# Retention stage of a decoder trunk: order and queues of its loads, and the place of the first output tile of its projection

## The chip, the core and the metric

The kernel runs on one core of one Trainium2 chip. The metric is the device time of one execution in microseconds (us), lower is better; a median of several executions is compared with that of the kernel before.

## The reference

One inference step of two layers, a retention layer and a sliding-window attention layer, for a new prompt of 1024 tokens (model width 1024) and eight decode tokens with stored states. The change lies in the retention layer: 4 heads, query and key width 256, value width 512, cut into 8 chunks of 128 tokens. Everything is float32.

```python
def retention_scan(q, k, v, S0):
    ...
    dmask = jnp.where(dist[None] >= 0, jnp.exp(log_g[:, None, None] * jnp.maximum(dist, 0.0)[None]), 0.0)
    cross_decay = jnp.exp(log_g[None, :] * (idx[:, None] + 1.0))
    k_decay = jnp.exp(log_g[None, :] * (C - 1.0 - idx[:, None]))
    chunk_decay = jnp.exp(log_g * C)
    ...
    def step(S, inp):
        qc, kc, vc = inp
        inner = jnp.einsum('bthd,bshd->bhts', qc, kc) * dmask[None]
        o = jnp.einsum('bhts,bshe->bthe', inner, vc) \
            + jnp.einsum('bthd,bhde->bthe', qc, S) * cross_decay[None, :, :, None]
        S_new = S * chunk_decay[None, :, None, None] \
            + jnp.einsum('bshd,bshe->bhde', kc * k_decay[None, :, :, None], vc)
        return S_new, o
    ...

def retention_layer(x, S0, g_norm, w_in, g_out, w_out):
    ...
    proj = h @ w_in
    q, k, v, gate = jnp.split(proj, [RET_QK, 2 * RET_QK, 2 * RET_QK + RET_V], axis=-1)
    ...
    o, S = retention_scan(q, k, v, S0)
    o = rmsnorm(o, g_out.reshape(RET_HEADS, RET_DV)).reshape(B, L, RET_V)
    o = o * jax.nn.silu(gate)
    return x + o @ w_out, S.astype(S0.dtype)
```

The attention layer that follows, and the decode tokens (one token each, with their own state), are left out here; neither is computed in another way after the change.

## The kernel before, in words

Float32 products run on TensorE as three matmuls each: every operand is split into a high part (a copy rounded to the matrix format, by ScalarE or VectorE) and a low part (the rest, by VectorE or GpSimd), and hi x hi, hi x lo and lo x hi are summed in PSUM. So each loaded tile has a conversion in front of its matmuls.

**Stage A** computes the input projection of the retention layer, set by set (queries, keys, values, gate, per head), and writes the results to three DRAM scratch tensors: `qks` (queries and keys, transposed), `vsc` (values) and `gsc` (gate). The output tiles pass through a small ring of SBUF buffers, `ring(key)`, with the keys `p`, `x`, `c`, `w` (the names `evp`, `evx`, `evc`, `evw` in the profile); `out_of` (line 346) takes one. The last set is a gate set; its spills are the last writes to `gsc`. The decode tokens' state work runs alongside. The order of ACT, DVE, POOL and SP is written by hand: work is entered with a time or a slot number and sorted, and `later(n, fn)` puts `fn` at slot `n` of the list. `b_first` (line 750) is entered five slots before the end and issues the first loads of stage B.

**Stage B** is the chunkwise retention. Its 32 steps are 4 heads x 8 chunks, two heads side by side: `steps` runs over the pair (0, 1), chunk by chunk, head by head, then over the pair (2, 3). So step 14 and 15 are the last chunk of heads 0 and 1, and steps 16 and 17 the first of heads 2 and 3; this is called the change of heads. A step `i` is spread over several iterations of the loop at line 1010:

- loads, all on SP (the SyncE queue): `b_q` (queries and keys, into ring `p`), `b_v` (values, ring `x`), `b_g` (gate, rings `c` and `w` by turns), 256 KB each; for step i+2 in iteration i, `b_q` ahead of the other work, `b_v` and `b_g` behind it
- `b_qk` (PE): scores and the transposed keys into the PSUM tile `tr`; in iteration i-1
- `others`: ScalarE's `kh`, `sTh`, `vh` (high parts of keys, scores, values), VectorE's `kl`, `sT`, `qh`, GpSimd's `vl`, `sTl`, `ql` for step i+1; the state's parts `Sh` (ACT, line 933) and `Sl` (DVE) from PSUM for step i-1; the norm of the output of step i-1 (ACT square, DVE and POOL for the root, DVE `on`); the gated output of step i-2 (`og`, then its high part into `A_hi` or `B_hi` and its low part)
- `b_mm` (PE, line 905): the matmuls of step i: the state (`S`, two PSUM tiles per head, lines from 913) and the output (`po`, up to line 926)
- `b_tr` (PE): four transposes of the normalised output `on` of step i-1 (printed as L100, the line of the helper)

At the last chunk of a head `b_Sh` writes the scaled state into an SBUF tile `sf` and stores it to the output on SP (line 938). The output norm's gain row of a head, `gbh`, is loaded by `gbl` (line 989) on SP into one of two buffers: heads 0 and 1 ahead of the loop together with the masks `M23`, heads 2 and 3 in iterations 14 and 15. In iteration 4 four VectorE operations (lines 1025 to 1028) multiply the decode tokens' output by their gate and split it.

**The output projection** (`ro_part`, `ro_finish`, from line 1114) follows. Output tile `ft` is 128 of the 1024 output columns for 512 tokens (`gi` 0) or 256 and 264 tokens (`gi` 1 and 2); it sums over 16 blocks of 128 rows of `w_out_ret`, in two halves `kh`, with 3 matmuls per block. The weights come in slots of 1024 x 256, so one slot serves one half of two neighbouring output tiles: `wslot` (line 1057) loads it on SP in two loads of 512 KB into `wr`, DVE makes `wh` (line 1071), POOL `wl` (line 1072); there are three slots' buffers and `ro_ahead` says how far ahead they are made. `ro_finish` loads the residual rows `xr` on SP, adds them on PE by four transposes into the same PSUM tile, and ACT copies the sum out and squares it for the next norm. The PSUM and SBUF pools of stage B are closed before the projection begins, so its buffers lie in the same memory, and a first write into such a buffer waits for the last reader of what lay there.

## Time and profile before

| what | value |
|---|---|
| median of 3 runs | 1365.36 us (1364.91 to 1365.54) |
| profiled execution, its own time | 1366.37 us |
| its span in the profile | 1364.6 us |
| mean granted TensorE clock | 0.99 |
| PE busy | 1313.3 us (96%) |
| DVE, ACT, POOL busy | 699.7, 629.5, 708.1 us |
| DMA | 186.63 MB, 137 GB/s over the span |

Durations in the text are of the profiled execution and count from the span's start. The engines are PE (TensorE matmul), PEld (its weight loads, beside PE), DVE (VectorE), ACT (ScalarE), POOL (GpSimd) and SP (SyncE, which only issues DMAs here; SPq and ACTq are the queues' issue instructions). In a row of the timeline stand the start, the duration, the engine, the line, the operation, the output and the inputs, and, in brackets, how long the engine had been idle before and what ended that. In a row of the windows stand the stretch and its length, then the busy time of PE (with the number of matmuls that began), PEld, DVE, ACT and POOL, the granted clock as a share of full speed, the DMA engines' share, and GB/s. A row of the groups ends in the busy time, the mean duration in ns and the idle time ahead.

### The profile page before, as it was taken

Reading aid. Unit: us, or ns where it says so; the run is one execution under the profiler, and the core shown is the slowest. Engines: PE = TensorE matmul, PEld = TensorE weight load, DVE = VectorE, ACT = ScalarE, POOL = GpSimd, SP = SyncE. Lnnn points to the kernel's source line nnn. Section 1 sums busy time; section 2 is a strip of 40 time slices with the busy share of each in tenths; the row PEclk is TensorE's granted clock in tenths of the full one; section 3 lists DMA queues with packets and bytes.
Section 4 is the critical chain, followed back from the end, with each engine's and each line's share of the span. In section 5 each row is a group of like instructions: output and inputs, shape, how many; then the busy total and the mean of one; then the engine's idle time right before and its main releaser. Section 6 shows DMA issues by size and latency. Waiting matters only on the chain.

```text
span 1364.6 us, 25935 instructions
## 1 busy us (share of the span) xinstructions
PE 1313.3 (96%) x9661; PEld 1225.7 (90%) x9661; DVE 699.7 (51%) x1361; ACT 629.5 (46%) x1561; POOL 708.1 (52%) x825
## 2 busy tenths in 40 slices
PE   6999999999999999897979999998999999999998
PEld 6999999999999999686868889997898999998998
DVE  6943655556556653675751112335555555669321
ACT  5532544545456543575740112244466666656311
POOL 6653525435445443697986553544476666545000
PEclk9999999999999999899989999999999999999999
DMA  6314677577667743565545354442112111103523
GB/s 219 102 55 144 209 234 220 173 225 232 197 213 219 219 147 98 182 174 197 169 148 170 113 158 129 127 129 79 47 47 63 48 43 34 48 30 100 166 81 82
DMA packets 192659, 186.63 MB, mean 137 GB/s; under 512 B 12581, under 2 KB 172381, under 8 KB 192517
## 3 DMA queue, kind: packets, MB, share of 16 engines
q1 hardware_dynamic: 155840, 148.87, 35.9%
q10 hardware_dynamic: 36692, 36.11, 8.5%
q8 instruction: 76, 1.25, 0.4%
q14 instruction: 51, 0.41, 0.1%
HBM read 128.56 MB, written 57.41 MB: 136 GB/s over the span
## 4 chain that ended last, share of the span: by engine, by line
PE 85%; DVE 5%; DMA 3%; POOL 3%; issue 2%; ACT 1%; SPq 0%; ACTq 0%; POOLq 0%; DVEq 0%
PE b L330 7%; PE b L332 7%; PE b L331 7%; PE pj L1082 6%; PE pj L1084 6%; PE pj L1083 6%; PE pj L1133 5%; PE pj L1131 4%; PE pj L1132 4%; PE b L323 4%; PE b L324 4%; PE b L325 4%; PE tr L100 4%; PE o L1546 2%; PE sc L1508 1%
## 5 line engine op out<-in xcount | busy, mean ns | idle before, releaser
L330 PE MATMUL b<-xh,woh 128*128 128x258 f32 x784 | 223.3, 285 | 0.0
L332 PE MATMUL b<-xh,wol 128*128 128x258 f32 x784 | 221.6, 283 | 0.0
L331 PE MATMUL b<-xl,woh 128*128 128x258 f32 x784 | 221.2, 282 | 0.0
L1082 PE MATMUL pj<-A_hi,wh 128*128 128x384 f32 (+1 forms) x512 | 178.1, 348 | 0.0
L1084 PE MATMUL pj<-A_hi,wl 128*128 128x384 f32 (+1 forms) x512 | 164.7, 322 | 0.0
L1083 PE MATMUL pj<-A_lo,wh 128*128 128x384 f32 (+1 forms) x512 | 164.6, 321 | 0.0
L330 PEld LDWEIGHTS b<-xh,woh 128*128 128x128 f32 x784 | 148.0, 189 | 4.1 <-issue 2.5
L331 PEld LDWEIGHTS b<-xl,woh 128*128 128x128 f32 x784 | 148.8, 190 | 0.0
L332 PEld LDWEIGHTS b<-xh,wol 128*128 128x128 f32 x784 | 148.1, 189 | 0.0
L221 POOL TENSOR_TENSOR wol<-raw,woh 128x512 fp32r<-128x512 f32 x52 | 68.5, 1325 | 139.1 <-ACT woh L216 138.3
L1072 POOL TENSOR_TENSOR wl<-wr,wh 128x1024 fp32r<-128x1024 f32 (+1 forms) x60 | 115.2, 1932 | 44.0 <-DVE wh L1071 21.7
L324 PE MATMUL b<-wol,xh 128*128 128x256 f32 x448 | 126.1, 281 | 0.4 <-DVE wol L221 0.4
L323 PE MATMUL b<-woh,xh 128*128 128x256 f32 x448 | 126.3, 282 | 0.0
L325 PE MATMUL b<-woh,xl 128*128 128x256 f32 x448 | 125.7, 281 | 0.0
L1082 PEld LDWEIGHTS pj<-A_hi,wh 128*128 128x128 f32 x512 | 97.0, 189 | 10.1 <-issue 9.4
L1083 PEld LDWEIGHTS pj<-A_lo,wh 128*128 128x128 f32 x512 | 97.2, 190 | 0.0
L1084 PEld LDWEIGHTS pj<-A_hi,wl 128*128 128x128 f32 x512 | 96.6, 189 | 0.0
L1523 POOL TENSOR_TENSOR s<-s,sm 128x512 f32<-128x512 f32 x64 | 68.9, 1077 | 48.4 <-DVE sm L1522 46.5
L323 PEld LDWEIGHTS b<-woh,xh 128*128 128x128 f32 x448 | 84.3, 188 | 2.5 <-issue 1.2
L324 PEld LDWEIGHTS b<-wol,xh 128*128 128x128 f32 x448 | 84.3, 188 | 0.8 <-DVE wol L221 0.8
L325 PEld LDWEIGHTS b<-woh,xl 128*128 128x128 f32 x448 | 84.3, 188 | 0.0
L1515 ACT ACTIVATE s<-s,mx 128x257 f32<-128x257 f32 x128 | 64.0, 502 | 31.6 <-DVE mx L1513 27.9
(357 smaller groups left out, 3569.6 us busy)
## 6 DMA issues: line engine op xcount, KB each, us to landing
raw<-in_w_in_ret_dram ACTq DMA_DIRECT2D x44, 512.0 KB
st<-in_state_ret_dram SPq DMA_DIRECT2D x64, 256.0 KB
out_dram<-st SPq DMA_DIRECT2D x64, 256.0 KB
wr<-in_w_out_ret_dram SPq DMA_DIRECT2D x32, 512.0 KB
wr<-in_w_in_swa_dram SPq DMA_DIRECT2D x18, 512.0 KB
vb<-vscr SPq DMA_DIRECT2D x64, 128.0 KB
evp<-qks SPq DMA_DIRECT2D x32, 256.0 KB
evx<-vsc SPq DMA_DIRECT2D x32, 256.0 KB
```

The lines of the kernel that those rows point to most:

```text
L221: eng.tensor_tensor(lo, src_of(s, name, sub), hi.bitcast(F32), SUB)
L323: mm(dst, xh, wh, start=a and i == 0, stop=False, skip_group_check=True)
L324: mm(dst, xh, wl, start=False, stop=False, skip_group_check=True)
L325: mm(dst, xl, wh, start=False, stop=z, skip_group_check=True)
L330: mm(dst, wh, xh, start=a, stop=False, **sg)
L331: mm(dst, wh, xl, start=False, stop=False, **sg)
L332: mm(dst, wl, xh, start=False, stop=z, **sg)
L1072: lo_eng[0].tensor_tensor(lo[:, js, :], raw[:, i:i + step, :], hi.bitcast(F32)[:, js, :], ALU.subtract)
L1082: mm(ps, hi[:, k, fs], xh[:, k, t0:t1], start=first and k == ks[0], stop=False)
L1083: mm(ps, hi[:, k, fs], xl[:, k, t0:t1], start=False, stop=False)
L1084: mm(ps, lo[:, k, fs], xh[:, k, t0:t1], start=False, stop=last and k == ks[-1])
L1523: nc.gpsimd.tensor_tensor(st[:, :, 0:256], st[:, :, 0:256], sm.unsqueeze(2).broadcast_to([128, 2, 256]), ALU.mult)
```

## The change

Five things change, line numbers being those of the changed kernel unless said otherwise.

1. The output tiles of the last gate set are taken from the buffers of the raw weights, so the ring is free then. `b_first` is entered ten slots before the end of the list instead of five, and loads the queries, values and gate of steps 0 and 1 and the queries of step 2.
2. In the loop `b_q` loads step i+3, one further ahead, and `b_v` (still i+2) is issued right behind it, ahead of `others`; `b_g` stays behind.
3. The store of the final state, and the gain rows of heads 2 and 3, are issued by ScalarE; the gain rows in iterations 16 and 17.
4. The four operations on the decode tokens' gate stand in iterations 4, 5, 6 and 7, one in each (`dec_gate`, line 1038).
5. The output tile `ft` 0, `gi` 0 of the projection is computed within stage B. `b_w` (line 1001) loads its 128 columns of `w_out_ret` in four loads of 256 KB on SP into ring buffers `p` and `x` in iterations 29 to 31, `b_wc` converts them (ACT high, DVE low), and `b_wmm` issues 12 matmuls for each, 48 in all: 24 ahead of the transposes of step 31, 24 behind them. The sum lies in one of the buffers of the state's PSUM tiles, which now have a pool of their own, `sSp`, that stays open until this tile is finished. Tiles 1 and on are computed as before, but tile 1 takes its two halves in the other order.

Three places, as the two programs have them. The first is SP at the end of stage A and the start of stage B; the `M` names are masks, `gsc<-ev..` or `gsc<-raw` the last gate spills. Before:

```order
L751 DMA M_84<-const_c_dram 128x256
L752 DMA M_84<-const_c_dram 128x36
L735 DMA evp<-qks 128x512
L742 DMA evx<-vsc 128x512
L735 DMA evp<-qks 128x512
L748 DMA evc<-gsc 128x512
L387 DMA gsc<-evw 128x2x128 x2
L387 DMA gsc<-evx 128x2x128 x2
L387 DMA gsc<-evp 128x2x128 x2
L991 DMA gbh<-in_ret_out_norm_dram 128x512
L742 DMA evx<-vsc 128x512
L748 DMA evw<-gsc 128x512
```

The same place after:

```order
L751 DMA M_84<-const_c_dram 128x256
L752 DMA M_84<-const_c_dram 128x36
L735 DMA evp<-qks 128x512
L742 DMA evx<-vsc 128x512
L748 DMA evc<-gsc 128x512
L735 DMA evp<-qks 128x512
L742 DMA evx<-vsc 128x512
L748 DMA evw<-gsc 128x512
L735 DMA evp<-qks 128x512
L387 DMA gsc<-raw 128x2x128 x8
L996 DMA gbh<-in_ret_out_norm_dram 128x512 x2
L1051 DMA M_7407<-const_c_dram 128x256
```

Seven loads of steps 0 to 2 now stand ahead of the last spills, before there were four; both gain rows and `M23` stand behind the spills.

The second place is the change of heads: SP before,

```order
L748 DMA evc<-gsc 128x512
L991 DMA gbh<-in_ret_out_norm_dram 128x512
L735 DMA evp<-qks 128x512
L938 DMA out_dram<-sf 128x2x512
L742 DMA evx<-vsc 128x512
L748 DMA evw<-gsc 128x512
```

and ACT after:

```order
L943 DMA out_dram<-sf 128x2x512
L957 ACTIVATE on,bss<-po 128x512
L891 ACTIVATE vh<-evx 128x512
L988 ACTIVATE B_hi<-og 128x4x128
L866 ACTIVATE kh<-tr,M_84 128x256
L881 ACTIVATE sTh<-sT 128x128
L996 DMA gbh<-in_ret_out_norm_dram 128x512
L942 ACTIVATE sf<-S 128x512 x2
```

The gain row and the store of the state left SP's queue, where loads stood behind them, for ACT's, where the square of the output norm (L957) and the conversions stand behind them.

The third place is SP at the end of stage B, with what each waits for (the other engines' names are those whose work must be done, DMAHW is an earlier transfer). Before:

```order
L938 DMA out_dram<-sf 128x2x512 [waits DMAHW5_49,Activation_49]
L1064 DMA wr<-in_w_out_ret_dram 128x4x256 [waits DMAHW6_49,DVE_49,PE_49]
L1064 DMA wr<-in_w_out_ret_dram 128x4x256 [waits DMAHW7_49,DVE_49,PE_49]
L1143 DMA xr<-in_x_prompt_dram 128x4x128 [waits DMAHW4_49,DMAHW5_49,DMAHW0_49,Pool_49]
L1143 DMA xr<-in_x_prompt_dram 128x4x128 [waits DMAHW1_49]
```

The same place after (`evp` and `evx` from `w_out_ret` are the weights of the first output tile):

```order
L1004 DMA evp<-in_w_out_ret_dram 128x4x128 [waits DMAHW3_49,PE_49,Pool_49]
L748 DMA evw<-gsc 128x512 [waits DMAHW4_49,DVE_49]
L1004 DMA evp<-in_w_out_ret_dram 128x4x128 [waits PE_49,Pool_49]
L1004 DMA evx<-in_w_out_ret_dram 128x4x128 [waits DMAHW6_49,DMAHW0_49,Activation_49]
L1004 DMA evx<-in_w_out_ret_dram 128x4x128 [waits DMAHW7_49,DMAHW2_49,Pool_49]
L1114 DMA wr<-in_w_out_ret_dram 128x4x256 [waits DVE_49,PE_49]
L1114 DMA wr<-in_w_out_ret_dram 128x4x256 [waits DMAHW3_49,DVE_49,PE_49]
L1191 DMA xr<-in_x_prompt_dram 128x4x128 [waits DMAHW1_49,DMAHW0_49,DMAHW4_49,PE_49,Pool_49]
L1191 DMA xr<-in_x_prompt_dram 128x4x128 [waits DMAHW5_49]
```

Four small weight loads stand among the last loads of stage B, and the first load of `xr` now waits for PE as well.

The diff:

```diff
@@ -348,7 +348,7 @@
         if s.kind == "v":
             c[key, t] = ring(key)[:, 0:512]
         elif t == 0:
-            r = ring(key).rearrange("p (t n) -> p t n", t=2)
+            r = (raw_tile()[:, 0:516] if s is sets[-1] else ring(key)).rearrange("p (t n) -> p t n", t=2)
             c[key, 0], c[key, 1] = r[:, 0], r[:, 1]
         return c[key, t]
 
@@ -752,9 +752,12 @@
         nc.sync.dma_start(out=M01[:, 256:292], in_=a["c1"][:, 640:676])
         b_q(0)
         b_v(0)
+        b_g(0)
         b_q(1)
-        b_g(0)
-    later(len(slots) - 5, b_first)
+        b_v(1)
+        b_g(1)
+        b_q(2)
+    later(len(slots) - 10, b_first)
 
 
     dve.memset(warm, 0.0)
@@ -840,6 +843,8 @@
         return [t.rearrange("p a b -> p (a b)").rearrange("p (k t) -> p k t", k=16) for t in (A_hi, A_lo, A_hif)]
 
     spp = sb.enter_context(tc.tile_pool(name="spp", bufs=1, space=PSUM))
+    ss_ = ExitStack()
+    sSp = ss_.enter_context(tc.tile_pool(name="sSp", bufs=1, space=PSUM, side="right"))
     M23 = rp.tile([128, 256], F32, name="M23")
     maskT = [M01[:, 0:128], M01[:, 128:256], M23[:, 0:128], M23[:, 128:256]]
     kdec = M01[:, 256:288].rearrange("p (h c) -> p h c", h=H)
@@ -906,7 +911,7 @@
         d = heads[h]
         kh, kl, vh, vl, sh, sl = [d.pop((x, c)) for x in ("kh", "kl", "vh", "vl", "sh", "sl")]
         if c == 0:
-            d["S"] = [spp.tile([128, DV], F32, tag="S", bufs=4, name="S") for _ in range(2)]
+            d["S"] = [sSp.tile([128, DV], F32, tag="S", bufs=4, name="S") for _ in range(2)]
         S = d["S"]
         for f in range(2):
             fs = slice(f * 128, f * 128 + 128)
@@ -935,7 +940,7 @@
             sf = rp.tile([128, 2, DV], F32, tag="Sh", bufs=2, name="sf")
             for f in range(2):
                 act(sf[:, f], d["S"][f], AF.Copy, scale=GAM[h] ** SREF)
-            nc.sync.dma_start(out=nrp[0, 0, h].rearrange("(f p) e -> p f e", p=128), in_=sf)
+            nc.scalar.dma_start(out=nrp[0, 0, h].rearrange("(f p) e -> p f e", p=128), in_=sf)
 
     def b_Sl(h, c):
         d = heads[h]
@@ -986,11 +991,39 @@
         _, ol, ohf = o_at(h, c)
         pool.tensor_tensor(ol, heads[h].pop(("og", c)), ohf, SUB)
 
-    def gbl(h):
+    def gbl(h, eng):
         t = rp.tile([128, DV], F32, name="gbh", bufs=2)
-        nc.sync.dma_start(out=t, in_=ret_out_norm[0, h * DV:h * DV + DV].partition_broadcast(128))
+        eng.dma_start(out=t, in_=ret_out_norm[0, h * DV:h * DV + DV].partition_broadcast(128))
         heads[h]["gb"] = t
 
+    wo = {}
+
+    def b_w(i):
+        t = ring("px"[i // 2])[:, 0:512].rearrange("p (k f) -> p k f", k=4)
+        nc.sync.dma_start(out=t, in_=w_out_ret[i * 512:i * 512 + 512, 0:128].rearrange("(k p) f -> p k f", p=128))
+        wo[i] = t
+
+    def b_wc(i):
+        raw = wo[i]
+        hi, lo = [rp.tile([128, DV], F32R, tag=("wo" if i < 2 else "v") + x, name="wo" + x, bufs=2)
+                  .rearrange("p (k f) -> p k f", k=4) for x in "hl"]
+        act(hi, raw, AF.Copy)
+        dve.tensor_tensor(lo, raw, hi.bitcast(F32), SUB)
+        wo[i] = hi, lo
+
+    def b_wmm(i):
+
+        if i == 0:
+            wo["ps"] = sSp.tile([128, 512], F32, tag="S", bufs=4, name="S")
+        hi, lo = wo[i]
+        xh, xl, _ = o_view(0)
+        for k in range(4):
+            kt = 4 * i + k
+            mm(wo["ps"], hi[:, k, :], xh[:, kt, 0:512], start=(kt == 0), stop=False)
+            mm(wo["ps"], hi[:, k, :], xl[:, kt, 0:512], start=False, stop=False)
+            mm(wo["ps"], lo[:, k, :], xh[:, kt, 0:512], start=False, stop=False)
 
     def at_step(fn, i):
         if 0 <= i < len(steps):
@@ -1002,30 +1035,47 @@
                       (b_kl, i + 1), (b_sh, i + 1), (b_vl, i + 1), (b_ol, i - 2), (b_sl, i + 1), (b_ql, i + 1)):
             at_step(fn, n)
 
-    gbl(0)
-    b_v(1)
-    b_g(1)
-    gbl(1)
+    def dec_gate(n):
+        if n == 0:
+            dve.tensor_tensor(gdec, gdec, odT, MUL)
+        elif n == 1:
+            dve.tensor_tensor(gdec, gdec, gcol[:, 0:16].unsqueeze(2).broadcast_to([128, 16, ND]), MUL)
+        elif n == 2:
+            dve.tensor_copy(B_hi[:, :, 512:520], gdec)
+        else:
+            dve.tensor_tensor(B_lo[:, :, 512:520], gdec, B_hif[:, :, 512:520], SUB)
+
+    NS = len(steps)
+    gbl(0, nc.sync)
+    gbl(1, nc.sync)
     nc.sync.dma_start(out=M23, in_=a["c1"][:, 384:640])
-    for i in range(-1, len(steps) + 2):
+    for i in range(-1, NS + 2):
         at_step(b_qk, i + 1)
         if i >= 0:
             at_step(b_mm, i)
         if i >= 0:
-            b_q(i + 2)
+            b_q(i + 3)
+            b_v(i + 2)
+        if i in (NS - 3, NS - 2):
+            b_w(i - NS + 3)
+        if i in (NS - 2, NS - 1):
+            b_w(i - NS + 4)
+        if i in (16, 17):
+            gbl(i - 14, nc.scalar)
         others(i)
+        if i == NS:
+            b_wmm(0)
+            b_wmm(1)
         at_step(b_tr, i - 1)
         if i >= 0:
-            b_v(i + 2)
             b_g(i + 2)
-        if i in (14, 15):
-            gbl(i - 12)
-        if i == 4:
-
-            dve.tensor_tensor(gdec, gdec, odT, MUL)
-            dve.tensor_tensor(gdec, gdec, gcol[:, 0:16].unsqueeze(2).broadcast_to([128, 16, ND]), MUL)
-            dve.tensor_copy(B_hi[:, :, 512:520], gdec)
-            dve.tensor_tensor(B_lo[:, :, 512:520], gdec, B_hif[:, :, 512:520], SUB)
+        if 4 <= i < 8:
+            dec_gate(i - 4)
+        for n in {NS - 2: (0,), NS - 1: (1, 2), NS: (3,)}.get(i, ()):
+            b_wc(n)
+        if i == NS:
+            b_wmm(2)
+            b_wmm(3)
     sb.close()
     se.close()
 
@@ -1095,13 +1145,11 @@
     iop = ctx.enter_context(tc.tile_pool(name="iop", bufs=1))
     acc = iop.tile([128, NT], F32, name="acc")
     fp = p2.enter_context(tc.tile_pool(name="fp", bufs=1))
-    ps2 = p2.enter_context(tc.tile_pool(name="ps2", bufs=4, space=PSUM))
-
     ro_slots = {}
-    ro_ps = {}
+    ro_ps = {(0, 0): wo["ps"]}
     RG = [(0, 512), (512, 768), (768, NT)]
 
-    ro_seq = [(half, fp_, kh) for half in range(2) for fp_ in range(4) for kh in range(2)]
+    ro_seq = [(half, fp_, kh if half + fp_ else 1 - kh) for half in range(2) for fp_ in range(4) for kh in range(2)]
 
     def ro_ahead(n):
 
@@ -1111,14 +1159,14 @@
 
     O_hi, O_lo, _ = o_view(0)
 
-    def ro_part(ft, gi, kh, pool):
+    def ro_part(ft, gi, kh, pool, first):
 
         t0, t1 = RG[gi]
         n = t1 - t0
         key = (min(gi, 1), ft // 2, kh)
         ro_ahead(ro_seq.index(key) + 1)
         hi, lo = ro_slots[key]
-        if kh == 0:
+        if first:
             ro_ps[ft, gi] = pool.tile([128, 512], F32, tag="pj", name="pj")
         ps = ro_ps[ft, gi][:, :n]
         fs = slice(ft % 2 * 128, ft % 2 * 128 + 128)
@@ -1128,7 +1176,7 @@
                 xh, xl = O_hi[:, kt, 0:512], O_lo[:, kt, 0:512]
             else:
                 xh, xl = B_hi[:, kt, t0 - 512:t1 - 512], B_lo[:, kt, t0 - 512:t1 - 512]
-            mm(ps, hi[:, k, fs], xh, start=(kt == 0), stop=False)
+            mm(ps, hi[:, k, fs], xh, start=(first and k == 0), stop=False)
             mm(ps, hi[:, k, fs], xl, start=False, stop=False)
             mm(ps, lo[:, k, fs], xh, start=False, stop=False)
             yield 3 * n / 2400.0
@@ -1184,18 +1232,24 @@
             nc.vector.tensor_scalar(e9[:n, c0:c1_], r9[:n, c0:c1_], EPS, None, ALU.mult)
             rsq(r9[:n, c0:c1_], r9[:n, c0:c1_], c1_ - c0)
 
+    ro_ahead(2)
+    ro_finish(0, 0)
+    ss_.close()
+    ps2 = p2.enter_context(tc.tile_pool(name="ps2", bufs=4, space=PSUM))
     npool = 0
-    for ft in range(8):
-        drain(ro_part(ft, 0, 0, ps2 if npool % 3 else pjp))
+
+    def ro_tile(ft, gi):
+        nonlocal npool
+        for n, kh in enumerate((1, 0) if (ft, gi) == (1, 0) else (0, 1)):
+            drain(ro_part(ft, gi, kh, ps2 if npool % 3 else pjp, n == 0))
         npool += 1
-        drain(ro_part(ft, 0, 1, None))
-        ro_finish(ft, 0)
+        ro_finish(ft, gi)
+
+    for ft in range(1, 8):
+        ro_tile(ft, 0)
     for ft in range(8):
         for gi in (1, 2):
...
+            ro_tile(ft, gi)
...
```

More of the change, by code (lines that the diff above doesn't have):

```diff
@@ L1185, in rstd9 @@
             rsq(r9[:n, c0:c1_], r9[:n, c0:c1_], c1_ - c0)
+    ro_ahead(2)
+    ro_finish(0, 0)
+    ss_.close()
+    ps2 = p2.enter_context(tc.tile_pool(name="ps2", bufs=4, space=PSUM))
     npool = 0
-    for ft in range(8):
-        drain(ro_part(ft, 0, 0, ps2 if npool % 3 else pjp))
+    def ro_tile(ft, gi):
+        nonlocal npool
+        for n, kh in enumerate((1, 0) if (ft, gi) == (1, 0) else (0, 1)):
+            drain(ro_part(ft, gi, kh, ps2 if npool % 3 else pjp, n == 0))
         npool += 1
-        drain(ro_part(ft, 0, 1, None))
-        ro_finish(ft, 0)
+        ro_finish(ft, gi)
+    for ft in range(1, 8):
+        ro_tile(ft, 0)
     for ft in range(8):
         for gi in (1, 2):
-            drain(ro_part(ft, gi, 0, ps2 if npool % 3 else pjp))
-            npool += 1
-            drain(ro_part(ft, gi, 1, None))
-            ro_finish(ft, gi)
+            ro_tile(ft, gi)
         if ft >= 1:
```

## The prediction

> **What bounds the kernel now.** I read the page's busy times first, then the windows, the matmul engine's timeline in the retention stage and at its end, and last the rows of SP (which issues the loads), ACT, DVE and POOL around each gap. The page's first rows:

> ```profile
> PE 1313.3 (96%) x9661; PEld 1225.7 (90%) x9661; DVE 699.7 (51%) x1361; ACT 629.5 (46%) x1561; POOL 708.1 (52%) x825
> ```

> TensorE is busy 96% of the span, so time can only come out of its few gaps, or out of stretches at a lower clock. The windows (columns PE, PEld, DVE, ACT, POOL busy, granted clock, DMA share, GB/s) show where they are in the retention stage, 543 to 702 us:

> ```profile
> 552.00:562.00 10.00, 9.14 (x36) 7.80 (x37) 6.17 (x14) 6.08 (x15) 4.57 (x8) 0.66 0.62 199
> 592.00:602.00 10.00, 10.00 (x57) 8.42 (x56) 7.66 (x18) 6.79 (x17) 9.44 (x12) 1.00 0.59 176
> 622.00:632.00 10.00, 6.58 (x35) 5.16 (x33) 3.35 (x8) 4.64 (x12) 5.21 (x7) 1.00 0.48 167
> 632.00:642.00 10.00, 6.08 (x35) 5.15 (x35) 6.51 (x15) 6.62 (x18) 6.82 (x9) 1.00 0.85 304
> ```

> In a normal stretch (592) PE is full and POOL next with 94%. Three places differ: the start, with a clock of 0.66; the change of heads at 622 to 642, with PE 63% busy; and the seam to the output projection. The PE timeline (start, duration, tile, idle time before it and what ended it) gives them, and a smaller gap at 578, one by one:

> ```profile
> 548.05 0.40 PE L919 MATMUL po<-vh,sTl 128*128 128x512 f32 x1
> 552.86 1.19 PE L854 MATMUL tr<-evp 128*128 128x128 f32 x4 [4.41 <-DMA evp<-qks]
> 559.48 0.48 PE L913 MATMUL S<-vh,kh 128*128 128x512 f32 x1
> 564.03 0.48 PE L913 MATMUL S<-vh,kh 128*128 128x512 f32 x1
> ...
> 573.19 0.48 PE L913 MATMUL S<-vh,kh 128*128 128x512 f32 x1
> 578.75 0.63 PE L100 MATMUL tr<-ident,on 128*128 128x128 f32 x4 [1.84 <-DVE on L964]
> 579.80 0.48 PE L913 MATMUL S<-vh,kh 128*128 128x512 f32 x1
> ...
> 621.01 0.47 PE L913 MATMUL S<-vh,kh 128*128 128x512 f32 x1
> 628.59 0.68 PE L854 MATMUL tr<-evp 128*128 128x128 f32 x4 [3.42 <-DMA evp<-qks]
> 635.27 0.68 PE L854 MATMUL tr<-evp 128*128 128x128 f32 x4 [3.27 <-DMA evp<-qks]
> 639.98 0.48 PE L913 MATMUL S<-vh,kh 128*128 128x512 f32 x1
> ...
> 702.39 0.63 PE L100 MATMUL tr<-ident,on 128*128 128x128 f32 x4
> 706.14 1.09 PE L100 MATMUL tr<-ident,on 128*128 128x128 f32 x4 [3.11 <-DVE on L964]
> 710.65 0.77 PE L1131 MATMUL pj<-A_hi,wh 128*128 128x512 f32 x1 [3.43 <-DVE wh L1071]
> 727.26 0.48 PE L1131 MATMUL pj<-A_hi,wh 128*128 128x512 f32 x1
> 738.86 0.48 PE L1131 MATMUL pj<-A_hi,wh 128*128 128x512 f32 x1
> ```

> The first L913 of a step marks it: 564.03 to 573.19 are two undisturbed steps of 4.58 each. An output tile of the projection is 727.26 to 738.86, 11.60, of which the four transposes at its end are 0.35, so 48 matmuls are 11.25.

> **Start of the stage.** Before, the chunk-2 queries (b_q(2)) are issued only inside the loop, and PE waits 4.41 for them, then works at the low clock. The change has them in flight some 10 us earlier, so this wait goes. Next late are the values of step 2, b_v(2). SP's issues, and ACT's wait for these values, before:

> ```profile
> 547.23 0.43 SPq L735 DMA_DIRECT2D evp<-qks  x1
> 547.76 0.38 SPq L742 DMA_DIRECT2D evx<-vsc  x1
> ...
> 553.49 0.63 ACT L886 ACTIVATE vh<-evx 128x512 fp32r<-128x512 f32 x1 [0.36 <-DMA evx<-vsc]
> ```

> They landed 5.7 us after their issue, at the end of a burst of seven loads. After the change they still stand behind gbh, gbh, M23 and b_q(3), and the first gbh must wait until the last gate spill has landed, since its buffer lies where that spill is read from (some 2 us later than now). Two 256 KB loads fewer stand ahead (v1 and g1), 0.84 each at the 304 GB/s of the table. So 2 later and 1.7 sooner: about 553 again. From there ACT needs 0.63 for vh and some 0.5 for kh, POOL 1.3 for vl: step 2 starts at 554.5 with a pause at its second matmul, instead of 559.48; what the following step keeps, with ACT running behind, I put at **4.4**. Ends: 6 (the values land with b_q(3), at 552) and 1.5 (PE's pauses between 551 and 555 bring the low clock again).

> **Decode gate.** The four DVE operations of step 4 now come one in each of steps 4 to 7. The step 573.19 to 579.80 took 6.61 against 4.58: 2.03 lost. The longest of the four:

> ```profile
> L1026 DVE TENSOR_TENSOR gdec<-gdec,gcol 128x128 f32<-128x128 f32 x1 | 1.3, 1256 | 0.0
> ```

> DVE is 7.66 of 10 busy, so it has 1.07 free per step. This one exceeds that by 0.2 and I leave 0.4 as lost; the others fit. **1.6**, ends 0.5 and 2.0.

> **Change of heads.** Here SP's queue is what was late. It stops after 616.76 until the gain row's buffer is free, and everything queues behind that and behind the state's store (sf):

> ```profile
> 616.76 0.32 SPq L748 DMA_DIRECT2D evc<-gsc  x1
> 623.80 0.33 SPq L991 DMA_DIRECT2D gbh<-in_ret_out_norm_dram  x1
> 624.24 0.37 SPq L735 DMA_DIRECT2D evp<-qks  x1
> 624.70 0.39 SPq L938 DMA_DIRECT2D out_dram<-sf  x1
> 625.18 0.42 SPq L742 DMA_DIRECT2D evx<-vsc  x1
> ...
> 625.18 5.28 DMA evx<-vsc
> ```

> (The last row is the chain's own: 5.28 from issue to use.) With gbh and the stores on ACT's queue, SP goes on as buffers come free. What is next late is ACT. In a normal step it starts when PE has done the step's matmuls, and the normalised output is ready 3.97 later (619.63):

> ```profile
> 615.66 1.09 ACT L933 ACTIVATE Sh<-S 128x512 fp32r<-128x512 f32 x2 [1.23 <-PE po L926]
> 618.88 0.75 DVE L964 SCALAR_TENSOR_TENSOR on<-po,bss,gbh 128x512 f32<-128x512 f32 x1 [0.44 <-POOL bss L115]
> ...
> 728.01 0.36 ACTq L1166 DMA_DIRECT2D xscr<-x  x1
> ```

> An issue on ACT is 0.36 (last row), and two stand in it for each of the two steps. Step 15's matmuls end at 624.57, as now; plus 3.97 and an issue the output of step 15 is there at 628.9; transposes and the scores of step 18 are 1.0 (step 17 at 629.9); the next output, with ACT busy to 628.8, at 632.8, and step 18 at 633.8 instead of 639.98. That is 6.2; I take 0.4 off for data that comes late among 1 MB of stores and 0.5 MB of gains: **5.8**. Ends: 6.5 and 3 (DMA full at 304 GB/s: 1.5 MB are 5 us of it). The same issue ahead of the square costs 0.3 at steps 15 and 31: **-0.6**. [...]

> **Seam.** Of the first tile's 48 matmuls nothing is new but their place: 11.25 of PE work goes into the time in which PE waited. From 702.39: transposes of step 30 (0.4), 24 matmuls, transposes of step 31 (0.4; their input, at 706, is no longer late), 24 matmuls: 714.45. Their weights come from four 256 KB loads (512 KB each for the other slots), converted by 4 ACT operations of 0.6 and 4 on DVE of 0.7, in the 1.2 that ACT waits per step and DVE's free time; the last is there by 707, its use is at 711.6. But the residual rows (xr) of this tile are loaded into memory that holds the last weights: in the built program SP waits for the last of the 48 matmuls. How long a 256 KB load takes alone, the last two loads of the stage bound:

> ```profile
> 690.64 0.32 SPq L748 DMA_DIRECT2D evw<-gsc  x1
> ...
> 692.90:693.60 0.70, 0.70 (x4) 0.56 (x3) 0.70 (x2) 0.00 (x0) 0.70 (x1) 1.00 0.05 18
> 693.60:699.70 6.10, 6.10 (x35) 5.15 (x34) 4.50 (x10) 4.37 (x11) 5.81 (x7) 1.00 0.01 3
> ```

> After 693.6 the DMA is idle, so 3.0 at most. PE stands from 714.45 to 717.45, then 0.35: tile 1 begins at 717.8 instead of 727.26, 9.45 sooner. Its weights: POOL may write the first low half only when the same 48 matmuls are done, and each later slot follows this cycle:

> ```profile
> 713.45 0.37 SPq L1064 DMA_DIRECT2D wr<-in_w_out_ret_dram  x1
> 717.01 0.69 DVE L1071 CAST wh<-wr 128x1024 fp32r<-128x1024 f32 x1 [5.80 <-DMA wr<-in_w_out_ret_dram]
> 717.84 2.38 POOL L1072 TENSOR_TENSOR wl<-wr,wh 128x1024 fp32r<-128x1024 f32 x1 [2.11 <-DVE wh L1071]
> ```

> 3.56 + 0.7 + 2.4 is 6.7 per slot, while tiles 1 and 2 use a slot in 5.6 each. First slot 716.85, then 723.5, 730.2 and 736.9; PE asks at 718.3, 723.9, 729.9 and 735.8: 0.3 and 1.1 of waiting, 1.2 with what overlaps. **8.2**; ends 9.5 (xr in 2.5, no wait for weights) and 5.

> On the clock: the pauses of 4.41 and 3.43 were followed by slow matmuls, that of 3.11 too (1.09 for the transposes, against 0.63), those of 3.42 and 3.27 not. A pause of 3.0 may thus go either way; at half clock for some 3.4 us it costs 1.7, held in the low end. [...]

> Sum: 4.4 + 1.6 + 5.8 - 0.6 + 8.2 = 19.4. The profiled execution took 1366.37 (span 1364.6), 1.0 over the median of the three runs, 1365.36; 1347.0 on its own time is **1346.0** beside the median.

> **Rivals.** (1) The loads order: in the loop b_q(i+3) now stands ahead of b_v(i+2) on SP, and waits for ql of step i on POOL. Before, these values went 2.6 us sooner. From ql to ql two steps on: issue 0.35, landing L, vh 0.64, then 3.7 of POOL work: L + 4.7, and two steps are 9.16. So it decides from L = 4.5. With 3.0 (the bound above) plus 0.4 for the load ahead it costs nothing; with the 5.28 of the chain's row 14 pairs lose 0.8 each, 11 in all, 1357; from L = 5.9 the gain is gone, and at 6.3 the kernel takes 1371, slower. The DMA share of 0.59 in a normal stretch speaks against such L. 7 in 100, of which slower 4, no change 2. (2) DMA full at the change of heads and the values late at the start: 1.5 and 3 there, 13.7 in all, 1351.7. For it speaks the 0.85 share at 632; against it that loads and stores now have 8 us more to spread over. 14 in 100. (3) Seam bound by xr and the weight slots, with the clock down: 4 there, 15.2 in all, 1350.2. For it speaks POOL's 2.38 per half slot; 11 in 100. That the 48 matmuls don't fill the gap, because their weights come late, I count in here.

> **How the numbers follow.** The forecast has 68 in 100. All high ends together give 23.4 (1342), all low ends 9.4 (1356); I take 1341 to 1354, which leaves out the slow case of (1) and the worst sums. Within 0.2% (2.7 us) is about what a measurement of this kernel can tell from no change. Faster 0.93, same 0.03, slower 0.04.

> **What would show it.** Right: no PE wait for evp at the start, but one of 1 to 2 for vh or vl before step 2; steps 15 to 18 in 12.8 instead of 18.97; a PE wait of about 3 for xr after the last wo matmul, and POOL wl as the releaser of short waits in tiles 1 and 2. Wrong: steps longer than 4.58 in undisturbed stretches with ACT vh waiting for evx (then rival 1), a low clock after the xr wait, or ACT waiting in its issues.

## The result, and the profile after

The changed kernel took 1350.99 us (median of 4 runs, 1349.63 to 1355.10) against 1365.29 us for the kernel before in the same comparison (4 runs, 1364.91 to 1365.54): 14.3 us less by the medians. The ratio of all runs is 0.9901, 95% interval 0.9879 to 0.9922. The forecast was 1346.0 with a range of 1341 to 1354. The profiled execution took 1350.44 (span 1348.6), 15.9 less than that of before. The page:

```profile
PE 1308.8 (97%) x9661; PEld 1222.4 (91%) x9661; DVE 701.1 (52%) x1365; ACT 633.6 (47%) x1565; POOL 707.4 (52%) x825
```

The matmul engine's timeline after, the rows that answer to those of before; L918 now marks a step, L1024 to L1026 are the early output tile, and the transposes of xr end an output tile:

```profile
543.33 0.68 PE L859 MATMUL tr<-evp 128*128 128x128 f32 x4 [0.56 <-issue]
546.73 0.50 PE L918 MATMUL S<-vh,kh 128*128 128x512 f32 x1 [1.83 <-ACT kh L866]
...
554.98 0.48 PE L918 MATMUL S<-vh,kh 128*128 128x512 f32 x1
559.55 0.48 PE L918 MATMUL S<-vh,kh 128*128 128x512 f32 x1
...
614.47 0.47 PE L918 MATMUL S<-vh,kh 128*128 128x512 f32 x1
622.38 0.63 PE L100 MATMUL tr<-ident,on 128*128 128x128 f32 x4 [1.02 <-DVE on L969]
627.50 0.63 PE L100 MATMUL tr<-ident,on 128*128 128x128 f32 x4 [1.76 <-DVE on L969]
628.55 0.47 PE L918 MATMUL S<-vh,kh 128*128 128x512 f32 x1
...
691.79 0.48 PE L1024 MATMUL S<-A_hi,woh 128*128 128x512 f32 x1
706.70 1.09 PE L100 MATMUL S<-ident,xr 128*128 128x128 f32 x4 [3.12 <-DMA xr<-in_x_prompt_dram]
719.79 0.60 PE L100 MATMUL pj<-ident,xr 128*128 128x128 f32 x4
729.69 0.50 PE L1181 MATMUL pj<-A_hi,wl 128*128 128x512 f32 x1 [0.46 <-POOL wl L1122]
732.12 0.60 PE L100 MATMUL pj<-ident,xr 128*128 128x128 f32 x4
```

Three marks of before that the prediction does not show, from the same view (step 31's first matmul is 698.78 there, and 687.37 after):

```profile
544.02 0.68 PE L854 MATMUL tr<-evp 128*128 128x128 f32 x4 [0.57 <-issue]
698.78 0.48 PE L913 MATMUL S<-vh,kh 128*128 128x512 f32 x1
750.11 0.60 PE L100 MATMUL pj<-ident,xr 128*128 128x128 f32 x4
```

The wait of 4.41 at the start is gone, the two of 3.42 and 3.27 at the change of heads became 1.02 and 1.76 and wait for VectorE, and the 48 matmuls fill the gap at the seam up to one pause of 3.12. From mark to mark, the profiled time is spent so:

| stretch | before | after | gain |
|---|---|---|---|
| up to stage B's first transposes | 544.0 | 543.3 | 0.7 |
| start: from there to step 3 | 20.0 | 16.2 | 3.8 |
| steps 3 to 15 | 57.0 | 54.9 | 2.1 |
| change of heads: steps 15 to 18 | 19.0 | 14.1 | 4.9 |
| steps 18 to 31 | 58.8 | 58.8 | 0.0 |
| seam: step 31 to the end of tile 2 | 51.3 | 44.8 | 6.6 |
| the rest, untouched by the change | 614.5 | 616.5 | -2.0 |

### The profile page after: what moved, and what is told of

It reads as the page before. It is cut to its first block, busy times and chain, and to the rows that moved or that the text cites. A ratio compares the mean times of both kernels' runs of the same rounds, so it can differ in the third digit from the quotient of the medians.

```text
span 1348.6 us, 25951 instructions
## 1 busy us (share of the span) xinstructions
PE 1308.8 (97%) x9661; PEld 1222.4 (91%) x9661; DVE 701.1 (52%) x1365; ACT 633.6 (47%) x1565; POOL 707.4 (52%) x825
## 4 chain that ended last, share of the span: by engine, by line
PE 85%; DVE 5%; POOL 4%; issue 3%; DMA 2%; ACT 1%; ACTq 0%; SPq 0%; POOLq 0%; DVEq 0%
PE b L330 7%; PE b L332 7%; PE b L331 7%; PE pj L1132 7%; PE pj L1134 6%; PE pj L1133 6%; PE b L323 4%; PE b L324 4%; PE b L325 4%; PE tr L100 4%; PE pj L1181 4%; PE pj L1179 4%; PE pj L1180 4%; PE o L1600 2%; POOL wl L1122 1%
```

## The experiments

Twelve kernels ran, four at a time on one chip beside the kernel before, whose median was 1367.9, 1367.1 and 1366.6 us in the three groups. Each median is to be set against that of its own group. The intervals are 2 to 3 us either way, and that is as much as many of these edits are worth; so each verdict rests on the lengths of the stretches as well. Where the code is the same, steps 3 to 15 repeat to 0.1, the start to 0.7, the seam to 0.9 and the change of heads to 1.3 (13.4 to 14.7), and a difference within that shows nothing. All were worked out as in the table above, from rows of the same view (us; bold where the edit acts):

| kernel | start | steps 3-15 | heads | seam | median | ratio to before (95%) |
|---|---|---|---|---|---|---|
| changed | 16.2 | 54.9 | 14.1 | 44.8 | 1350.99 | 0.9901 (0.9879 to 0.9922) |
| changed, again | 16.5 | 55.0 | 14.7 | 45.6 | 1351.71 | 0.9887 (0.9870 to 0.9904) |
| loads put back | **19.1** | 54.9 | **14.8** | 45.0 | 1355.71 | 0.9908 (0.9893 to 0.9923) |
| stores, gains on SP | 16.3 | 54.9 | **16.9** | 45.4 | 1356.40 | 0.9909 (0.9886 to 0.9931) |
| decode gate together | 16.4 | **57.0** | 13.4 | 44.7 | 1354.84 | 0.9906 (0.9888 to 0.9924) |
| no early tile | 16.4 | 54.9 | 13.5 | **50.1** | 1358.32 | 0.9927 (0.9908 to 0.9946) |
| early xr | 16.2 | 54.9 | 14.1 | **47.5** | 1355.88 | 0.9921 (0.9904 to 0.9937) |
| early xr, slots on ACT and DVE | 16.3 | 54.9 | 13.9 | **43.5** | 1349.77 | 0.9875 (0.9858 to 0.9891) |
| low parts on DVE alone | 15.8 | 55.0 | 13.5 | **44.1** | 1351.97 | 0.9897 (0.9879 to 0.9916) |
| norm first, gains on SP | 16.3 | 54.9 | **13.4** | 44.7 | 1354.03 | 0.9902 (0.9887 to 0.9917) |
| state parts moved, v2 sooner | **14.5** | 54.9 | 13.9 | 46.7 | 1350.54 | 0.9881 (0.9866 to 0.9896) |
| start and seam together | **13.1** | 54.9 | 13.4 | **45.8** | 1347.70 | 0.9861 (0.9840 to 0.9883) |
| start, seam and heads | **13.1** | 54.9 | **13.5** | **44.7** | 1347.73 | 0.9862 (0.9840 to 0.9883) |

### Each part undone

The theory was that every part pays at its own place; the rivals, that one part carries another's gain. First the loads (values and gate of step 1 go back between the two gain rows as well).

```diff
-            r = (raw_tile()[:, 0:516] if s is sets[-1] else ring(key)).rearrange(...)
+            r = ring(key).rearrange(...)
         b_v(0)
-        b_g(0)
         b_q(1)
-        b_v(1)
-        b_g(1)
-        b_q(2)
-    later(len(slots) - 10, b_first)
+        b_g(0)
+    later(len(slots) - 5, b_first)
...
-            b_q(i + 3)
-            b_v(i + 2)
+            b_q(i + 2)
...
+            b_v(i + 2)
             b_g(i + 2)
```

> The changed kernel with its loads put back: last gate set in the ring again, first loads five slots before the end, b_q(i+2) ahead of and b_v(i+2) behind the other work. The rest of the change stays. Theory (each part pays in its own place): only the start is lost, 4.5 us (step 2 began at 559.48 before and at 554.98 after), so about 1355.5 against the changed kernel's 1351.0, and the low clock after the start comes back. Rival (the deeper loads carry the change of heads too): PE waits for evp again at step 17 or 18, 3 us more, about 1358.5.

The start lost 2.9 us of the 4.5 expected. PE's timeline of this kernel has the old wait again, and its slow transposes behind:

```profile
551.95 1.19 PE L856 MATMUL tr<-evp 128*128 128x128 f32 x4 [3.99 <-DMA evp<-qks]
```

The change of heads took 14.8, hardly beyond what kernels with the same code there show (13.4 to 14.7). So the loads' depth pays at the start, and the rival's 3 us elsewhere are not there.

```diff
-            nc.scalar.dma_start(out=nrp[0, 0, h]..., in_=sf)
+            nc.sync.dma_start(out=nrp[0, 0, h]..., in_=sf)
-        if i in (16, 17):
-            gbl(i - 14, nc.scalar)
+        if i in (14, 15):
+            gbl(i - 12, nc.sync)
```

> The changed kernel with the state's stores and the gain rows of heads 2 and 3 back on SP, the gains in iterations 14 and 15. Theory: the change of heads loses the 4.9 us that it gained (step 15 to 18 took 18.97 before, 14.08 after), about 1355.9. [...] Rival 2 (the deeper loads alone brought the gain): nothing lost, 1351.0.

The change of heads takes 16.9: 2.8 us of the 4.9 are lost, neither all of it, as the theory had it, nor nothing, as the rival of the deeper loads had it. What the rows show is a queue that stands still. SP's issues in this kernel, then ACT's wait for the values of step 17 and PE's behind it:

```profile
612.75 0.38 SPq L748 DMA_DIRECT2D evc<-gsc  x1
617.73 0.33 SPq L996 DMA_DIRECT2D gbh<-in_ret_out_norm_dram  x1
618.17 0.37 SPq L735 DMA_DIRECT2D evp<-qks  x1
618.64 0.37 SPq L742 DMA_DIRECT2D evx<-vsc  x1
...
623.56 0.63 ACT L891 ACTIVATE vh<-evx 128x512 fp32r<-128x512 f32 x1 [3.15 <-DMA evx<-vsc]
...
625.69 0.68 PE L859 MATMUL tr<-evp 128*128 128x128 f32 x4 [2.77 <-DVE kl L871]
```

The queue stops again from 613 to 617.7, and the values behind it come 3.15 too late for ACT; its kh and VectorE's kl stand behind that, and PE for kl. A slow window of the clock (626.82 to 630.23) follows PE's pause and is in the 2.8. The queries, for which PE waited in the kernel before, are in flight by then. The two parts share this gain and do not add: with the queue relieved and the loads put back the stretch took 14.8, 4.1 less than before; with the deeper loads and the old queue 16.9, 2.1 less; with both 14.1, 4.9 less.

```diff
-        if 4 <= i < 8:
-            dec_gate(i - 4)
+        if i == 4:
+            for n in range(4):
+                dec_gate(n)
```

> The changed kernel with the decode gate's four VectorE operations in iteration 4 again. Theory: 2.0 us lost (6.50 minus 4.48 between the traces), 1353.0, and one step of 6.6 us in the timeline. Rival (the loads come earlier now, so VectorE has slack at that place): nothing lost, 1351.0.

Steps 3 to 15 take 57.0 again, 2.0 more, with a wait at the same place as before, 1.87 for the normalised output:

```profile
574.73 0.63 PE L100 MATMUL tr<-ident,on 128*128 128x128 f32 x4 [1.87 <-DVE on L969]
```

Theory confirmed. The last part was undone by leaving out `b_w`, `b_wc` and `b_wmm` and computing tile 0 after the stage:

```diff
-    for ft in range(1, 8):
+    for ft in range(8):
         ro_tile(ft, 0)
```

> The changed kernel without the early output tile: no b_w, b_wc, b_wmm; tile 0 is computed after stage B as the others are. Theory: the seam loses 6.6 us (step 31 to tile 3: 17.97 minus 11.41), 1357.6; two pauses of 3.1 to 3.4 us come back, and with them three or four windows of 3.4 us at a clock of 0.5. Rival (the weight slots of tiles 1 and 2 bound the seam either way): at most 3 us lost, 1354.0.

The seam lost 5.3 us of the 6.6 expected, more than the rival's 3. The gaps that come back, on PE:

```profile
695.03 1.08 PE L100 MATMUL tr<-ident,on 128*128 128x128 f32 x4 [3.22 <-DVE on L969]
697.72 0.77 PE L1168 MATMUL pj<-A_hi,wh 128*128 128x512 f32 x1 [1.60 <-DVE wh L1110]
701.66 0.79 PE L1170 MATMUL pj<-A_hi,wl 128*128 128x512 f32 x1 [2.75 <-POOL wl L1111]
```

Matmuls of 0.77 to 0.79 instead of 0.40 to 0.48 lie in the slow windows that were expected: three, from 694.85 to 705.09. The early tile is worth 5.3; the other 1.3 of the 6.6 is not assigned (the kernel before had four slow windows at the seam, and one costs up to 1.7, by estimate, half of its 3.41).

Set against the kernel before in its own group, the four kernels gain 2.1, 2.8, 1.2 and 4.7 us less than the 14.3 of the changed kernel, in the order of the table.

### What the seam is bound by

The forecast had the pause for xr in its sum, and 1.2 us for waits for weights. Two theories for what it lost: the pause, or the weight slots.

```diff
+    def b_xr():
+        t = wo["xr"] = rp.tile([128, 4, 128], F32, tag="og", name="xr", bufs=2)
+        nc.sync.dma_start(out=t, in_=x_prompt[0, 0:512, 0:128]...)
         if i == NS:
+            b_xr()
             b_wmm(2)
             b_wmm(3)
+            for n in range(4):
+                tr(wo["ps"][:, n * 128:n * 128 + 128], wo["xr"][:, n, :], ident, start=False, stop=(n == 3))
```

> The changed kernel with the residual rows of tile 0 loaded during stage B into a buffer of the gated output, and their transposes right behind the 48 matmuls; so the pause of 3.12 us for xr goes. Theory A (that pause and the slow window behind it are what the seam lost against the forecast): tile 3 begins about 4 us sooner after the first early matmul. Theory B (the slots of weights bound tiles 1 and 2: GpSimd can write the first low half only after the 48 matmuls, and needs 2.4 us for each half): PE waits for wl in tiles 1 and 2 instead, and tile 3 begins at most 0.5 us sooner.

The pause went, and the seam grew by 2.7 us. PE's waits in this kernel:

```profile
706.17 0.50 PE L1188 MATMUL pj<-A_hi,wl 128*128 128x512 f32 x1 [1.40 <-POOL wl L1129]
712.64 0.50 PE L1186 MATMUL pj<-A_hi,wh 128*128 128x512 f32 x1 [1.10 <-DVE wh L1128]
715.08 0.50 PE L1188 MATMUL pj<-A_hi,wl 128*128 128x512 f32 x1 [1.70 <-POOL wl L1129]
729.17 0.50 PE L1188 MATMUL pj<-A_hi,wl 128*128 128x512 f32 x1 [1.41 <-POOL wl L1129]
```

Theory A falls, B holds and was too mild: the slots set the pace, and the second slot came later than in the changed kernel. Its first high half was cast at 709.48 there and at 711.90 here:

```profile
711.90 0.69 DVE L1128 CAST wh<-wr 128x1024 fp32r<-128x1024 f32 x1 [10.23 <-DMA wr<-in_w_out_ret_dram]
```

The load for it is issued at the same time (706.15; 705.85 in the changed kernel). But tile 0 finishes sooner, so its two stores (704.81 and 705.26) stand ahead of that load now, where in the changed kernel they came behind it (708.29 and 708.71); two loads of residual rows stand ahead in both. That the stores delayed it is argued from these times, not tried by itself.

```diff
+            hi_act[0], lo_eng[0] = (True, nc.vector) if len(ro_slots) < 4 else (False, nc.gpsimd)
             ro_slots[key] = wslot(...)
```

> The kernel of the run before, and the first four slots of weights converted by ACT (high part) and VectorE (low part) instead of VectorE and GpSimd. Theory B: 1.3 us for a low half instead of 2.4 brings what the earlier xr alone could not: tile 3 begins 2 to 4 us sooner than in the changed kernel. Theory A: no gain beyond that of the run before. A third bound (the loads of wr themselves, two buffers of 512 KB and 3.5 us each): 1 to 2 us sooner, with waits whose chain leads to wr.

With the early xr and the faster conversions the seam takes 43.5, 4.0 us less than in the run before, so theory A falls. Against the changed kernel it is 1.3 less: theory B had 2 to 4, the third bound, the loads, 1 to 2. PE's two waits are for `wh` now, and for the second of these ACT could begin only when the load had landed (712.71, after 5.00 of idling):

```profile
706.20 0.50 PE L1187 MATMUL pj<-A_hi,wh 128*128 128x512 f32 x1 [2.11 <-ACT wh L1126]
713.40 0.50 PE L1187 MATMUL pj<-A_hi,wh 128*128 128x512 f32 x1 [1.09 <-ACT wh L1126]
```

The last piece is a faster conversion without the early xr:

```diff
+            lo_eng[0] = nc.vector if len(ro_slots) < 4 else nc.gpsimd
             ro_slots[key] = wslot(...)
```

> The changed kernel with the low parts of the first four slots of weights on VectorE (not GpSimd); the residual rows of tile 0 come late as in the changed kernel. Theory (the pause for xr and the slots' chain lie side by side, so that removing one alone brings little): the pause of 3.1 us for xr stays, PE's wait for wl in tile 2 goes, and tile 3 begins 0.5 to 0.8 us sooner after the first early matmul. Rival (GpSimd's low halves alone are the bound): 2 us sooner.

```profile
705.93 0.63 PE L100 MATMUL S<-ident,xr 128*128 128x128 f32 x4 [3.17 <-DMA xr<-in_x_prompt_dram]
719.09 0.60 PE L100 MATMUL pj<-ident,xr 128*128 128x128 f32 x4
730.70 0.60 PE L100 MATMUL pj<-ident,xr 128*128 128x128 f32 x4
```

The pause stays and tile 2 has no wait left (11.61), as the theory said. The seam is 0.6 shorter, which lies within the spread of the same code, and the median doesn't show it; the rival's 2 us are not there.

### Start and change of heads

```diff
+    for nm in ("Sh", "Sl", "Sh", "Sl"):
+        rp.tile([128, 2, DV], F32R, name=nm, bufs=2)
+            if i == 0:
+                b_v(2)
+                gbl(1, nc.sync)
             b_q(i + 3)
+            if i == 0:
+                nc.sync.dma_start(out=M23, ...)
```

> The changed kernel with two things altered at the start of stage B: the buffers of the state parts are laid over the raw weights' buffers, so that the values' high part and the gain rows no longer wait for the landing of the last gate spill; and on SP b_v(2) goes right behind the first gain row, the second gain row and the masks M23 behind it. Theory: step 0 begins 2.0 us sooner, step 2 1.5 to 2.0 us sooner. Rival (step 2 stands for the landing of its values at the end of the burst of loads, which stays as long): step 0 sooner, step 2 not, no gain.

The start takes 14.5 instead of 16.2, 1.7 us less. Step 0 began 1.3 sooner (545.48) and step 2 2.6 sooner (552.37), but 1.1 of that went again behind step 2, where ACT waited 3.46 for the values of step 3. The two later kernels with these edits did not have that wait and took 13.1. But the seam is 2.0 longer. SP issues the first load of weight slots at 699.20 instead of 691.03, right after a matmul of the early tile; the author's reading of the program is that the moved buffers put the third and fourth early weights where this load goes. The residual rows stand behind it: PE waits 4.60 for them, and two slow windows follow. The two cancel nearly.

```diff
-            gbl(i - 14, nc.scalar)
+            gbl(i - 14, nc.sync)
-        for fn, n in ((b_og, i - 2), (b_Sh, i - 1), (b_Sl, i - 1), (b_sq, i - 1), (b_ts, i - 1), (b_pw, i - 1),
+        st = ((b_Sh, i - 1), (b_Sl, i - 1))
+        nm = ((b_sq, i - 1), (b_ts, i - 1), (b_pw, i - 1))
+        for fn, n in ((b_og, i - 2), *((nm + st) if i - 1 in (15, 16) else (st + nm)),
```

> The changed kernel with two things altered at the change of heads: the gain rows of heads 2 and 3 go out on SP in iterations 16 and 17 (not on ACT), and for steps 15 and 16 ACT and VectorE do the norm of the output ahead of the copies of the state. Theory (ACT's queue is the bound there: state copy, store issue, and the issue of the second gain row that stood 1.1 us for a transfer): step 15 to 18 takes 12.0 instead of 14.08, 2.0 us less. Rival (the transfers are the bound, 1.5 MB in that stretch): nothing gained, PE or VectorE wait for a DMA.

13.4 instead of 14.1, within the spread of the same code and far from 12.0: the theory falls. ACT's waiting was real in the profile that it was read from. ACT was done at 622.11, the issue of the second gain row stood in its queue until 623.33, and the state copy behind it:

```profile
623.33 0.35 ACTq L996 DMA_DIRECT2D gbh<-in_ret_out_norm_dram  x1
623.73 0.60 ACT L938 ACTIVATE Sh<-S 128x512 fp32r<-128x512 f32 x1 [1.61 <-PE tr L100]
```

But that wait belongs to this execution. In the eight other profiles with the same code there the issue stood 0.16 to 0.66. Where the decode gate was put back it stood 0.16, and steps 15 to 18 took 13.4 in the old order:

```profile
624.74 0.35 ACTq L996 DMA_DIRECT2D gbh<-in_ret_out_norm_dram  x1
625.14 1.08 ACT L938 ACTIVATE Sh<-S 128x512 fp32r<-128x512 f32 x2 [0.56 <-DVE kl L871]
```

With the issue gone from ACT, PE still stood for others. PE, then VectorE and GpSimd of the run with the norm first:

```profile
622.79 0.68 PE L859 MATMUL tr<-evp 128*128 128x128 f32 x4 [0.73 <-PE tr L100]
627.01 0.63 PE L100 MATMUL tr<-ident,on 128*128 128x128 f32 x4 [1.23 <-DVE on L969]
...
622.20 0.48 DVE L871 SCALAR_TENSOR_TENSOR kl<-tr,M,kh 128x256 fp32r<-128x256 f32 x1 [0.92 <-ACT kh L866]
624.87 1.34 DVE L902 CAST qh<-evp 128x256 fp32r<-128x256 f32 x1
626.13 0.74 DVE L969 SCALAR_TENSOR_TENSOR on<-po,bss,gbh 128x512 f32<-128x512 f32 x1
...
624.78 1.27 POOL L896 TENSOR_TENSOR vl<-evx,vh 128x512 fp32r<-128x512 f32 x1
```

PE goes on 0.11 after VectorE's kl is done (622.68), and that waited 0.92 for ACT's kh, which stands behind the state copy in either order (it ended 7.5 us after the start of step 15, and 7.4 in the changed kernel): the norm came sooner, the keys did not. The second wait is for an output that VectorE made late, since a copy of 0.28 took 1.34. So reordering ACT's queue only moved the wait; the rival, transfers, is not what these rows show either.

### The changed kernel again, and all together

> The changed kernel itself once more, as the measure for the three others on the same chip, and for how much its time moves by itself. Theory (the window grid of the clock lies anew against the program in each execution, so that a pause of 1.7 to 3.4 us is followed by a slow window in one execution and not in another): the number of slow windows differs from the first profile's 4, by one to three, at 1.0 to 1.7 us each, and the runs spread over 4 us or more. Rival (the differences come from the data transfers): the same windows as in the first profile, and other stages longer.

The runs spread over 2.6 us (1350.49 to 1353.14), less than the 4 expected, though the two groups together run from 1349.6 to 1355.1. The profile has 5 slow windows where the first had 4, one of them at the start and one at the change of heads, where the first had none. The change of heads is 0.6 longer, with that slow window in it. The seam is 0.8 longer without one: there the loads of weights took 3.78, 3.35 and 3.97 us from issue to cast, where they took 3.63, 3.32 and 3.44 in the first profile, so the transfers move a part of it too. What the start and the seam had pointed to was then put into one kernel (the third and fourth early weights in a buffer of `Sl`, beside the edits shown):

```diff
+            t = rp.tile([128, 2, DV], F32R, tag="Sl", name="wo", bufs=2)
+            hi, lo = t[:, 0], t[:, 1]
```

> The changed kernel with all that the runs point to at the start and the seam: state parts over the raw weights' buffers and b_v(2) ahead of the second gain row; the residual rows of tile 0 loaded in stage B; low parts of the first four slots on VectorE; and the third and fourth early weight pieces in the buffer of the state's low parts, so that no first slot of weights stands for the last early matmuls. Theory: 1.5 us at the start and 3 to 4 at the seam, 5 us less than the changed kernel on the same chip. Rival (the loads of wr bound the seam: two buffers, 3.5 us or more each): 1.5 and 2, 3.5 us less.

1347.70 (1346.36 to 1351.04) against 1351.71 for the changed kernel in the same group, 4.0 less, with intervals to the kernel before that overlap (0.9840 to 0.9883 and 0.9870 to 0.9904). The start gave 3.4, the seam nothing (45.8 against 45.6), so 4.0 is near the rival's 3.5 but not by its parts, 1.5 and 2. PE and SP at the seam (the last row spans four issues, the second of them at 702.45):

```profile
708.72 0.50 PE L1197 MATMUL pj<-A_hi,wh 128*128 128x512 f32 x1 [2.71 <-DVE wh L1138]
...
700.51 1.14 SPq L1211 DMA_DIRECT2D xr<-in_x_prompt_dram  x2
701.75 10.44 SPq L1131 DMA_DIRECT2D wr<-in_w_out_ret_dram  x4
```

The slot's buffer was free after 698.5 (the end of VectorE's first low half), but its load stands on SP behind the residual rows, which wait for PE's transposes of tile 0 at 699.85. Two slow windows follow PE's pause of 2.71. A kernel with the weights ahead of the residual rows was not tried.

> The kernel of the run before, and at the change of heads the gain rows on SP and the norm ahead of the state copy for steps 15 and 16, as in the run that altered these two alone. Theory (transfers bound the change of heads now; the profile of the run with these two alone had 13.4 for steps 15 to 18, kernels with the changed order 13.4 to 14.1): 0 to 0.7 us less than the run before, not to be told from it. Rival (ACT's order was worth its 1.1 us of waiting): 1.5 us less.

1347.73: not to be told from the run before, as the theory said.

## Why the prediction was right, and where it was off

The direction, most of the mechanisms and the range held; the gain was 14.3 us where 19.4 was forecast. In the profiled pair the stretches that the terms stand for gained 18.1.

**Start** (4.4): 4.5 by the step's own time (559.48 to 554.98), of which 0.7 already stood at the first transposes. Step 2 is late for its values, as forecast, and the price was right, since these values came last. What was not seen is that step 0 itself began later (546.73, against 545.87): ACT's vh lies on the raw buffers, so it waits for the last gate spill, and PE waits 1.83 for kh. ACT's vh of steps 0 and 2:

```profile
545.68 0.63 ACT L891 ACTIVATE vh<-evx 128x512 fp32r<-128x512 f32 x1 [2.00 <-DMA gsc<-raw]
552.71 0.63 ACT L891 ACTIVATE vh<-evx 128x512 fp32r<-128x512 f32 x1 [2.13 <-DMA evx<-vsc]
```

Moving those buffers, with b_v(2) sooner, gave 1.7 in one profile and 3.1 in the two of the later kernels.

**Decode gate** (1.6): 2.1. The 0.4 left as lost was not lost.

**Change of heads** (5.8, less 0.6 for the issues there and at step 31): 4.9. The sum had ACT's chain as what comes next, and so it was, with 14.1 for steps 15 to 18 instead of 12.8 (13.2 with the 0.4 that the term takes off). The step that failed is that an issue on ACT costs 0.36: the second gain row's stood in ACT's queue for 1.21 first. In the other profiles of this code, where it stood 0.16 to 0.66, the stretch took 13.4 to 14.1, or 14.7 with a slow window in it, so the term was too high by 0.2 to 0.9, and how much is chance of the execution. The low end of 3, for a DMA full at 304 GB/s, did not come: 4.9 were measured, and what went was a queue that stood still (before, SP issued nothing from 617.08 to 623.80).

**Seam** (8.2): 6.6, the term that was mis-sized most. The 11.25 of early matmuls, the pause for xr (3.12 against 3.0) and their order were as forecast, and so was the cycle of a slot: the first low halves of four slots ended 6.6 to 6.8 apart, against 6.7. But counted from step 31, tile 1 began 8.4 sooner and not 9.45: the first transposes came 0.4 later, and those of xr ran at half clock, 0.4 more. Tiles 1 and 2 then took 1.9 more than their 11.60 each, where the sum had 1.2 for weights. In the first profile only 0.46 of that is a wait for wl, and a slow window behind the pause (706.55 to 709.97, clock 0.50), which the sum left out, stands in its place. In the second profile, at full clock, PE waited 1.97 for wl in these tiles, and the seam took 45.6. The slots could not have fed PE sooner: take the pause away and PE waits for wl and wh instead. The reason given for the pause is in doubt, too. By the author's reading of the program, which no profile shows, the xr buffer does not overlap the last early weights; its pool takes over the memory of a closed pool, and its first write waits for that pool's last user. The traces agree with this: with tile 0's rows loaded early, into a buffer of the open pool (issued at 692.03), those rows did not wait, and the first xr load behind was issued 0.07 after the transposes that read them (704.37).

**What no term held**: 2.0 us in the rest, which the change doesn't touch. The rest goes with the slow windows in it: over the 14 profiles it took 614.5 to 616.9 with two, 616.5 to 617.5 with three and 617.2 to 619.0 with four; before has two there, after three. The profiled pair differs by 15.9, the medians by 14.3, since the profiled execution of before was 1.1 over its median and that of the changed kernel 0.5 under. Why is not shown; the other executions have no profile.

**Rivals.** By the number alone, 1350.99 is nearer to rival (2)'s 1351.7 and rival (3)'s 1350.2 than to 1346.0; it is the stretches that decide. (1) Steps 18 to 31 took 58.8 before and after, so the values behind the queries cost nothing. (2) A full DMA would have left 1.5 at the start and 3 at the change of heads; 4.5 and 4.9 were measured. (3) The seam bound by xr and the slots, with the clock down, is what happened, at 6.6, between its 4 and the forecast's 8.2.

## What to carry to other kernels

When a gap is filled, price what stands beside it: two waits that lie side by side are worth little singly (0.6 here for the one), and removing the visible one can cost time (seam 44.8 to 47.5), here, as far as the times show, by moving stores ahead of the load that counts. A transfer issued from a computing engine cost more than its issue here, since that issue could wait (0.35 for the second gain row's, after 1.21 in ACT's queue); look for what it waits for, and for what stands behind it. And compare stretches between marks in the profiles when edits are worth less than the runs' spread.
